# A hand-ordered mixer: weight halves ahead of state work on VectorE, SiLUs and a logarithm moved on ScalarE

## The chip, the core and the metric

One core of one Trainium2 chip. The metric is the device time of one execution in microseconds (us); less is better. Engines are named as in the profile: PE is TensorE's matmul side, PEld its weight loads, DVE is VectorE, ACT is ScalarE, POOL is GpSimd, SP is SyncE, which issues nearly all DMAs.

## What is computed

One decoder layer on 264 columns, 256 tokens of a prompt and 8 samples of one token each, with a model width of 2048: a half-step FFN, a mixer, another half-step FFN and a gated per-layer embedding, each with its norms. All of it is fp32. The change lies in the mixer:

```python
proj = u @ w_in                       # 2048 -> 81 column tiles of 128
glu_a, glu_b, z, xbc, dt_raw = split(proj)
v = glu_a * sigmoid(glu_b)            # conv group, 1024 channels
v = silu(layernorm(causal_dwconv(v, width 31)))
xbc = silu(causal_dwconv(xbc, width 4))
xs, B, C = split(xbc)                 # 8 groups, 6 heads each, state 128
dt = softplus(dt_raw + bias)
y, h_new = ssd(xs, dt, a, B, C, d_skip, h0)   # chunked scan, chunks of 128
y = rmsnorm(y * silu(z)) per group
mix = concat(v, y) @ w_out
```

For the 8 samples `ssd` is one step from a given state h0 (128 x 1024 fp32 for each third of a group): the output needs the product of the old state with C, summed over the state.

## The kernel before

**Matmuls and weights.** Activations lie with the channels on the partitions and the 264 columns along the free dimension. An fp32 product is made of three products in the rounded format fp32r: `mm3` (L449-454) issues high weight x high activation (L451), high weight x low activation (L452) and low weight x high activation (L453). Weights come in units of 8 tiles of 128x128, 512 KB: `Weights.load` (L303) issues one DMA on SP into `wraw` (L325), ScalarE copies it, rounding, into the high half `whi` (L328), and VectorE subtracts to get the low half `wlo` (L338). A column tile of the mixer takes two units, called n_0 and n_8, and 48 matmuls. `wraw`, `whi` and `wlo` have four buffers each, and loads are made two column tiles ahead. So a DMA into `wraw` waits for VectorE's low half of the unit two column tiles earlier, and a high copy waits until PE has done its last L452 of the unit two column tiles earlier. Accumulators are PSUM tiles `acc` (5 buffers); other PSUM tiles are `ps` (3 buffers).

**The mixer** (L805-1241) loops over `IN_ORDER` (L1153): dt first, then for each of the eight groups the tiles C, B, three x and three z, and, in between, pairs gb and ga of the conv group. Beside the weights' halves VectorE and ScalarE do:

- `do_conv` (L921-936): short conv of a B, C or x tile out of its accumulator; ScalarE takes the first tap, VectorE three more, ScalarE the SiLU (L936). It also collects the last columns in `xo`.
- `do_glu` (L952-972): the sigmoid as Exp, Ln, Exp on ScalarE (L957-959), a product on VectorE, and 30 long taps on VectorE (`y<-v,vec,y`, L418), four of them queued after each tile of the loop (L1238-1240).
- old-state work: `load_state` (L1037-1039) brings h0 through SP into one of two buffers; `state_times_c` (L1041-1047) multiplies it by C (`h<-h,cbc`, L415) and sums it (`ych<-h`, L1047). The next load into a buffer waits for that sum. `load_cbc` (L1033) brings C, spread over the partitions, into a single buffer.
- `load_sums` (L990-1008) brings the running sums of dt for a group into `ab` and `ea` through SP (L996); `decays` (L1012-1021) makes twelve Relus and three Exps of them on ScalarE; `decay_cb` (L1049) multiplies them on VectorE (`ab<-ab,rr`).
- `ssd` (L1060-1111): PE transposes x and B (L1070, L1071), VectorE scales them (`xdt`, `xde`), PE makes the chunk states (L1087) and the outputs (L1102). `ssd_samples` (L1114) does the samples.
- `gate_begin` (L1132): product with SiLU(z), three squares on ScalarE, two run additions on VectorE. `gate_end` (L1140-1147): PE sums over the partitions (L512), ScalarE takes the inverse root as Ln and Exp (`rsqrt`, L515-518), VectorE makes three outputs, and `split` (L456-465) makes of each a high half on ScalarE (L460) and a low half on VectorE (L461).
- the SiLU of a z tile (L1221) reads an accumulator and frees it. SiLU lies in another activation table than Ln and Exp; a change of table shows as ACT_TABLE_LOAD (L437).

**The order.** From the mixer's beginning on, each engine's order is written out by hand in `ISSUE` (L148-260): four lists, for PE, DVE, Activation and SP, of the engine's instructions by their place in the program. `issue_in_order` (L263-297) ties each instruction to the one before it in its list, without a semaphore. An engine works through its list in order, and an instruction that waits holds back all behind it.

## Time and profile before

| | us |
| --- | --- |
| time, median of 3 runs | 2380.87 |
| lowest and highest run | 2376.16, 2381.4 |
| the profiled execution | 2377.88 |
| its span | 2376.2 |
| PE busy in the span | 2355.9 |
| DVE busy | 1574.8 |
| ACT busy | 1187.7 |

The profile is one execution, and its times count from the start of the span; the mixer lies at about 822 to 1310 us. Rows of a timeline give the start, the duration of the group, engine and line, the operation with its tiles, how many follow one another, and in brackets the idle time before it and what ended it. A row of the waits names the engine and line that waited, the one that released it, the total, how often, and the longest. L-numbers are those of the kernel before.

### The profile page before, as it was taken

Reading aid. Unit: us, or ns where it says so; the run is one execution under the profiler, and the core shown is the slowest. Engines: PE = TensorE matmul, PEld = TensorE weight load, DVE = VectorE, ACT = ScalarE, POOL = GpSimd, SP = SyncE. Lnnn points to the kernel's source line nnn. Section 1 sums busy time; section 2 is a strip of 40 time slices with the busy share of each in tenths; the row PEclk is TensorE's granted clock in tenths of the full one; section 3 lists DMA queues with packets and bytes.
Section 4 is the critical chain, followed back from the end, with each engine's and each line's share of the span. In section 5 each row is a group of like instructions: output and inputs, shape, how many; then the busy total and the mean of one; then the engine's idle time right before and its main releaser. Section 6 shows DMA issues by size and latency. Waiting matters only on the chain.

```text
span 2376.2 us, 47323 instructions
## 1 busy us (share of the span) xinstructions
PE 2355.9 (99%) x19470; PEld 2335.6 (98%) x19470; DVE 1574.8 (66%) x2396; ACT 1187.7 (50%) x1791; POOL 184.7 (8%) x206
## 2 busy tenths in 40 slices
PE   9999999999999999999999999999999999999998
PEld 9999999999999999999999999999999999999998
DVE  6554455545556988989899965865545655565586
ACT  6444444433446576666565454644444443344465
POOL 1400000000006000000000011000000000000103
PEclk9999999999999999999999999999999999999999
DMA  7655555555555777666665556567766676676563
GB/s 261 218 185 181 185 183 182 184 183 184 184 171 184 232 240 227 211 226 208 226 215 188 185 170 230 186 239 244 237 202 228 232 245 212 214 237 207 180 207 126
DMA packets 163145, 489.34 MB, mean 206 GB/s; under 512 B 25280, under 2 KB 42736, under 8 KB 162928
## 3 DMA queue, kind: packets, MB, share of 16 engines
q1 hardware_dynamic: 160848, 485.27, 62.2%
q8 instruction: 152, 2.49, 0.4%
q10 hardware_dynamic: 2080, 1.04, 0.2%
q14 instruction: 65, 0.53, 0.1%
HBM read 465.65 MB, written 21.88 MB: 205 GB/s over the span
## 4 chain that ended last, share of the span: by engine, by line
PE 87%; DVE 7%; DMA 3%; ACT 2%; issue 1%; SPq 0%; ACTq 0%; DVEq 0%
PE acc L453 28%; PE acc L452 28%; PE acc L451 28%; DVE wlo L338 3%; DMA wraw<-in_w 2%; ACT whi L328 1%; DVE h L415 1%; PE ps L451 1%; PE ps L453 1%; PE ps L452 1%; DVE y L418 0%; DVE h L418 0%; PE ps L512 0%; PE ps L1102 0%; DMA ea<-d_cs 0%
## 5 line engine op out<-in xcount | busy, mean ns | idle before, releaser
L453 PE MATMUL acc<-act,wlo 128*128 128x264 f32 x6128 | 1733.5, 285 | 3.2 <-DVE wlo L338 3.2
L452 PE MATMUL acc<-act,whi 128*128 128x264 f32 x6128 | 1721.5, 282 | 1.8 <-DVE act L418 1.8
L451 PE MATMUL acc<-act,whi 128*128 128x264 f32 x6128 | 1704.4, 282 | 3.5 <-ACT whi L328 1.7
L338 DVE TENSOR_TENSOR wlo<-wraw,whi 128x1024 fp32r<-128x1024 f32 (+2 forms) x814 | 972.6, 1197 | 579.3 <-ACT whi L328 575.3
L328 ACT CAST whi<-wraw 128x1024 fp32r<-128x1024 f32 (+2 forms) x814 | 830.9, 1024 | 948.7 <-PE acc L452 662.4
L451 PEld LDWEIGHTS acc<-act,whi 128*128 128x128 f32 x6128 | 1147.1, 189 | 6.3 <-ACT whi L328 2.1
L453 PEld LDWEIGHTS acc<-act,wlo 128*128 128x128 f32 x6128 | 1145.6, 187 | 6.8 <-DVE wlo L338 4.8
L452 PEld LDWEIGHTS acc<-act,whi 128*128 128x128 f32 x6128 | 1147.1, 187 | 4.4 <-DVE act L418 2.2
L415 POOL TENSOR_TENSOR run<-run,tmp 128x264 f32<-128x264 f32 x77 | 72.9, 954 | 878.7 <-ACT tmp L442 878.3
L418 DVE SCALAR_TENSOR_TENSOR y<-v,vec,y 128x229 f32<-128x229 f32 (+21 forms) x240 | 106.9, 468 | 0.6
L418 DVE SCALAR_TENSOR_TENSOR s<-bb,xds,s 128x128 f32<-128x128 f32 x192 | 52.6, 346 | 69.7 <-POOL s L415 69.7
L415 POOL TENSOR_TENSOR s<-s,eap 128x1024 f32<-128x1024 f32 x24 | 46.4, 1935 | 630.6 <-DMA s<-in_hst 532.9
L415 DVE TENSOR_TENSOR tmp<-acc,rr 128x264 f32<-128x264 f32 x99 | 42.5, 430 | 48.9 <-PE acc L453 48.6
L460 ACT CAST act<-tmp 128x264 fp32r<-128x264 f32 x104 | 42.1, 410 | 63.0 <-DVE tmp L415 57.4
L415 DVE TENSOR_TENSOR tmp<-tmp,acc 128x264 f32<-128x264 f32 x84 | 35.9, 427 | 38.1 <-PE acc L453 37.9
L415 POOL TENSOR_TENSOR run<-run,y 128x264 f32<-128x264 f32 x7 | 8.4, 1207 | 582.9 <-ACT run L495 503.5
L415 DVE TENSOR_TENSOR y<-y,acc 128x264 f32<-128x264 f32 x80 | 34.0, 425 | 29.5 <-PE acc L453 29.5
L415 DVE TENSOR_TENSOR act<-tmp,act 128x264 fp32r<-128x264 f32 x122 | 52.9, 438 | 0.1
L453 PE MATMUL ps<-act,wlo 128*128 128x264 f32 x192 | 52.2, 284 | 0.0
L442 ACT ACTIVATE tmp<-tmp 128x264 f32<-128x264 f32 x112 | 46.9, 420 | 10.2 <-DVE tmp L415 9.9
L452 PE MATMUL ps<-act,whi 128*128 128x264 f32 x192 | 52.0, 282 | 0.0
L451 PE MATMUL ps<-act,whi 128*128 128x264 f32 x192 | 46.1, 282 | 0.0
(173 smaller groups left out, 1013.4 us busy)
## 6 DMA issues: line engine op xcount, KB each, us to landing
wraw<-in_w SPq DMA_DIRECT2D x755, 512.0 KB, 4.7
h<-in_hst SPq DMA_DIRECT2D x24, 512.0 KB, 8.1
s<-in_hst SPq DMA_DIRECT2D x24, 512.0 KB, 6.3
out_nss<-s SPq DMA_DIRECT2D x24, 512.0 KB, 2.6
wraw<-in_w SPq DMA_DIRECT2D x35, 256.0 KB, 3.8
wraw<-in_w SPq DMA_DIRECT2D x23, 384.0 KB, 7.3
ab<-d_cs SPq DMA_DIRECT2D x14, 384.0 KB, 5.5
cbc<-d_bc SPq DMA_DIRECT2D x8, 512.0 KB, 6.3
```

The source lines that it names most:

```text
L328: self.hi = nc.scalar.copy(hi, raw).ins
L338: nc.vector.tensor_tensor(out=lo, in0=raw, in1=hi.bitcast(F32), op=ALU.subtract)
L415: return (eng or nc.vector).tensor_tensor(out=out, in0=in0, in1=in1, op=op)
L418: return nc.vector.scalar_tensor_tensor(out=out, in0=in0, scalar=scalar, in1=in1, op0=op0, op1=op1)
L442: i = nc.scalar.activation(out=out, in_=in_, func=func, bias=bias, scale=scale)
L451: keep(nc.tensor.matmul(acc, hi, x[:, 0, :], start=first, stop=False))
L452: keep(nc.tensor.matmul(acc, hi, x[:, 1, :], start=False, stop=False))
L453: traced[0] = keep(nc.tensor.matmul(acc, lo, x[:, 0, :], start=False, stop=last)).ins
L460: nc.scalar.copy(t[:, 0, :], x)
```

## The change

Only two of the four lists in `ISSUE` change: DVE's (772 instructions) and Activation's (582). Each holds the same instructions as before in another order; PE's and SP's lists, buffers, tiles and arithmetic stay.

On DVE about seventy low weight halves move forward by 0.4 to 3.0 us of work, past products and sums of the old state, long taps and low halves of the gate's outputs. The sums and products that they pass come correspondingly later: for example sum 304 stands behind run addition 293 and low half 324 (173_8), where it stood ahead of 313, 316, 318 and 271; low half 440 (184_0) passes 381 and sum 417, but stays behind 379, the low half of the gate's first output; and the first `xde` of group 1 (141) passes 118, 120, 152 and 122.

On Activation two places change. In group 1 the first two z SiLUs (140, 143) go ahead of the table load 116 and of the copies and squares behind it, and the rsqrt (117, 118), table load 126 and third z SiLU (146) go ahead of the high copy of 161_8 (156). In group 4 the high halves of the gate's three outputs (299, 300, 301), which stood among the glu's Exp (308), the decays' Exps (318, 325, 326), table load 329 and high copies 340 and 341, go behind the high copy of 185_8 (347), and the SiLU 330 goes ahead of 341.

```diff
 "DVE":
-        57 76 60 81 83 74 77 80 59 61-62 89 82 90 84 91 94 85 78 111-112 63 113 116 64 131 92 95
-        86 79 132-133 136 114 154 93 65-66 96 67 87 134 137 115 155 99 98 173 88 135 68-69 156
-        159-160 174 107 100 164 70 157 175 108 101 158 176-177 109 102 110 103 127 104 138 161
-        128 178-179 105-106 180 129 181 184 162 188 130 182 189 163 150 183 123 125 117 119 121
-        166 165 151 139-140 124 126 190 193 118 120 152 122 141 202 191 153 203 192 171 204
...
+        57 76 60 77 80 59 61-62 81 83 89 74 90-91 94 78 111 82 112 84-85 63 113 116 64 131 92 79
+        132 95 86 133 136 114 154 93 65-67 134 115 155 96 87 99 98 173 137 135 68-69 156 159 174
+        88 160 107 100 164 70 157 175 108 101 158 176-177 109 102 110 103 127 104 138 161 178
+        128 179 105-106 180-181 184 188 129 162 182 189 130 163 150 183 123 125 117 119 121 166
+        165 151 139-140 124 126 190 193 141 202 118 120 191 203 152 122 192 204 153 171 142-143
...
-        245 256 300 250 342 246 257 301 251 311 264 252 265 253 266 292 267 312 303 317 323 270
-        304 313 316 318 271 293 314 324-325 328 349 329 272 294 315 350-351 354 326 355 330 273
...
+        300 250 342 246 301 251 311 257 264 252 265 253 266 292 267 312 303 317 323 313 316 293
+        314 324 270 304 325 328 349 318 294 315 350 271 329 272 351 354 326 355-356 330 273 352
...
-        376-377 402 404 395 400-401 396 399 410 397 378 380 382 411 416 398 412 415 379 388 403
-        405 381 417 413 440 383 441-442 445 431 389-390 414 450-451 443 391 456 430 444 392 457
...
+        376-377 396 399 410 400 397 378 380 382 411 401 416 398 412 415 379 388 403 405 413 440
+        381 441 417 442 445 431 389 414 450-451 383 390 443 456 391 430 444 392 457 418-419 393
...
-        435 482 493 458 474 483 485 459 494 499 486 460 495 498 500 475 461 505 496 476 464 506
...
+        426 448 427 471 449 428 472 479 452 432 524 453 433 480 454 434 481 484 435 482 493 455
+        474 483 494 458 485 459 499 495 498 475 505 486 460 496 476 506 500 507 510 497 531 461
...
 "Activation":
-        116 145 147 91-93 148-150 155-157 117-118 126 140 143 146 158 151 119-121 128 166 129
+        140 143 116 145 147 91-93 148-150 155 117-118 126 146 156-158 151 119-121 128 166 129
...
-        331 298 306 332-334 307 299 308 318 325 300 326 329 340 301 341-342 346 330 343 347 309
-        349 335 350 344 348 351-352 336-337 353-354 338 355-358 339 363 359 345 364-366 374-381
+        331 298 306 332-334 307-308 318 325-326 329 340 330 341-342 346 343 347 299-301 309 349
+        335 350 344 348 351-352 336-337 353-354 338 355-358 339 363 359 345 364-366 374-381
```

## The prediction, made before the changed kernel was run

> **What bounds the kernel now.** I read the page first, then the chain of waits of TensorE over the mixer, the only part whose orders change, then windows around each wait, then the instructions of VectorE, ScalarE and SP in those windows.

> ```profile
> PE 2355.9 (99%) x19470; PEld 2335.6 (98%) x19470; DVE 1574.8 (66%) x2396; ACT 1187.7 (50%) x1791; POOL 184.7 (8%) x206
> ```

> TensorE (PE) works 99% of a span of 2376.2 us, so no reordering on the other engines can win more than what TensorE now waits for. Which of it lies in the mixer, 822 to 1310 us, the waits say (engine, line, released by: us in total, times, longest):

> ```profile
> PE acc L453 <- DVE wlo L338: 2.5, 4, 0.9
> PE acc L451 <- ACT h L442: 1.6, 2, 1.3
> PE ps L1070 <- ACT tmp L442: 1.4, 1, 1.4
> PE ps L1070 <- ACT h L442: 1.3, 1, 1.3
> PE ps L512 <- DVE run L415: 0.4, 1, 0.4
> PE ps L1087 <- DVE xde L415: 0.4, 1, 0.4
> PE acc L451 <- ACT whi L328: 0.2, 1, 0.2
> ```

> They sum to 7.8 us, 0.33% of the time. That is the ceiling of any gain. Against it stands how full VectorE is where they lie (window, us, then busy us of PE, PEld, DVE, ACT, POOL, clock, DMA share, GB/s):

> ```profile
> 860.00:936.00 76.00, 72.52 (x589) 69.43 (x588) 74.31 (x130) 52.05 (x91) 0.00 (x0) 1.00 0.72 225
> ...
> 1003.00:1031.00 28.00, 27.28 (x226) 27.01 (x225) 28.00 (x49) 19.26 (x34) 0.00 (x0) 1.00 0.57 180
> ...
> 1063.00:1092.00 29.00, 26.99 (x224) 26.57 (x223) 28.41 (x47) 20.31 (x41) 0.00 (x0) 1.00 0.55 185
> ```

> VectorE is busy 74.31 of 76, 28.00 of 28 and 28.41 of 29 us. In these three stretches a microsecond that VectorE idles is a microsecond that everything behind it comes later, so a move is judged by one question: does the instruction that now comes first have its input?

> **The change, group by group.** Nothing is added or removed; each term is a wait that goes or a wait that comes. The sum is made on the profiled execution (2377.88 us), which is 3.0 below the median of the runs, 2380.87.

> *Group 1 (860 to 936).* Gain: the first two z SiLUs free their accumulators ahead of a table load, and the rsqrt stands ahead of a weight copy, so the waits of 1.4 (L1070) and 1.3 (L451) go, and the xde wait of 0.4 too. Loss: the low halves pushed forward stand ahead of the reduce that frees a state buffer.

> ```profile
> 887.46 1.21 DVE L1047 TENSOR_REDUCE ych<-h 128x8 f32<-128x1024 f32 x1
> ```
> ```profile
> 888.69 0.33 SPq L1039 DMA_DIRECT2D h<-in_hst  x1
> 890.62 0.97 SPq L996 DMA_DIRECT2D ab<-d_cs  x2
> ```
> ```profile
> 896.01 3.63 ACT L442 ACTIVATE ab<-ab,acs 128x128 f32<-128x128 f32 x12 [2.65 <-DMA ab<-d_cs]
> 899.54 1.04 ACT L328 CAST whi<-wraw 128x1024 fp32r<-128x1024 f32 x1
> ```
> ```profile
> 901.26 0.28 PE L451 MATMUL acc<-act,whi 128*128 128x264 f32 x1
> ```

> SP issues in order. The state load left at 888.69, right after the reduce ended at 888.67, and the ab loads behind it at 890.62. In the new order the work put ahead of the reduce, less that put behind, is 2.3 us. Low 132 (155_8) among it now also waits for weights that stand on SP behind another later state load, 1.4 us by my estimate (0 at least). The reduce ends near 892.5, the ab loads leave 2.3 later, since they had 1.6 us to spare behind the state load, and the twelve Relus, which already waited for them, start at 898.3. The copy behind them, high half 158_0, ends at 902.9 in place of 900.58. PE wants it at 901.26: +1.7, and VectorE, whose low 158_0 reads it, is 2.3 late. Then the moved high copy:

> ```profile
> 915.43 0.61 PE L512 MATMUL ps<-run,ones 128*128 128x264 f32 x2
> 915.87 0.61 PE L1054 MATMUL ps<-c,b 128*128 128x128 f32 x4
> ```
> ```profile
> 918.50 1.28 ACT L437 ACT_TABLE_LOAD   x1
> ```
> ```profile
> 918.36 1.22 DVE L338 TENSOR_TENSOR wlo<-wraw,whi 128x1024 fp32r<-128x1024 f32 x1
> ```

> The copy of 161_8 now stands behind the rsqrt, the table load and a SiLU. The rsqrt reads the sum of L512, which ends at 916.04 and so at 917.7 with PE 1.7 late; two steps of the rsqrt and a SiLU (some 0.4 each by my estimate, from the Relus' 12 in 3.63 and their longer tiles), 1.3 for the load and 1.04 for the copy give 921.3. Its low half starts there and not at 918.36: VectorE is now 2.9 late. The full stretch doesn't give it back before the second xde, whose work ahead is the same:

> ```profile
> 933.47 0.55 DVE L415 TENSOR_TENSOR xde<-xdt,dte 128x384 f32<-128x384 f32 x1
> ```
> ```profile
> 935.76 0.81 PE L1087 MATMUL ps<-xde,rr 128*128 128x384 f32 x2
> ```

> It ended at 934.02 and PE used it at 935.76, a slack of 1.74. With 2.9 it ends at 936.9, so **+1.2** at the end of the group, although the old waits are gone. Its bounds: with 0 in place of 1.4, the xde is only 1.5 late and the group gives 0.2 back; if nothing ahead is late, PE gains no more than the slack, −1.75; with another 0.5 of idle it is +1.75. I take +1.2.

> *Group 3 (1003 to 1031).* The low half 173_8 (VectorE 324) goes 3 us forward, past reduces, and would end the wait at 1010.94 (0.72 of the 2.5). But a run addition (293) stays ahead of it:

> ```profile
> 1008.05 0.72 ACT L442 ACTIVATE tmp<-h 128x264 f32<-128x264 f32 x2
> ```
> ```profile
> 1009.67 1.21 DVE L338 TENSOR_TENSOR wlo<-wraw,whi 128x1024 fp32r<-128x1024 f32 x1
> ```

> That addition reads the first of the two squares, done at about 1008.46. VectorE comes to it some 2.4 us earlier, once the reduces no longer stand before it, and idles. The low half ends near 1010.45 against 1010.88: 0.4 won of 0.7. The reduce that had let a state load go at 1007.07 (next fence) now comes behind it and one long tap: 0.4 and 1.2 more, so it ends at 1012.0. On it hangs the next state load, and on that, in SP's order, the weights:

> ```profile
> 1007.07 0.33 SPq L1039 DMA_DIRECT2D h<-in_hst  x1
> 1007.50 0.38 SPq L931 DMA_DIRECT2D out_xo<-xo  x1
> 1007.93 4.96 SPq L325 DMA_DIRECT2D wraw<-in_w  x3
> ```
> ```profile
> 1013.98 1.05 ACT L328 CAST whi<-wraw 128x1024 fp32r<-128x1024 f32 x1 [4.67 <-PE acc L453]
> ```
> ```profile
> 1017.62 0.28 PE L451 MATMUL acc<-act,whi 128*128 128x264 f32 x1
> ```

> Both move 4.9 us. The weights for 175_0 leave at 1012.9 instead of 1007.93. The copy began 6.05 after the issue, now at 1018.9, and ends at 1020.0 where PE wants it at 1017.62: **+2.4**. If they land in the median 4.7 us, it is +1.0; if the low half after it also queues behind a product that waits for the late state, +3.3.

> ```profile
> wraw<-in_w SPq DMA_DIRECT2D x755, 512.0 KB, 4.7
> ```

> [...]

> *Group 4 (1063 to 1092).* Gain: the SiLU that PE's transposes wait for (1.3) comes earlier, and low 184_0 (440) goes ahead of a reduce. But the three high copies of the gate (ScalarE 299 to 301, L460) now stand behind the high copy of 185_8 (347), and VectorE's subtraction (379) that reads the first of them still stands ahead of 440:

> ```profile
> 1078.39 0.28 PE L452 MATMUL acc<-act,whi 128*128 128x264 f32 x1
> ```
> ```profile
> 1076.17 0.42 DVE L415 TENSOR_TENSOR act<-tmp,act 128x264 fp32r<-128x264 f32 x1
> 1076.52 0.42 DVE L415 TENSOR_TENSOR v<-v,acc 128x264 f32<-128x264 f32 x1
> 1076.86 1.82 DVE L415 TENSOR_TENSOR ab<-ab,rr 128x768 f32<-128x768 f32 x2
> ```
> ```profile
> 1081.72 0.39 PE L453 MATMUL acc<-act,wlo 128*128 128x264 f32 x1 [0.74 <-DVE wlo L338]
> ```

> 347 writes the buffer that PE last reads at 1078.39, so it runs from about 1078.7 to 1079.7; the gate's copy (a quarter as wide: some 0.4 by estimate) ends at 1080.1. Only then do 379 (pitch 0.35), the v product (0.35), the two decay products (0.9 each), a conv tap (0.4) and low 440 (1.2) run: 1084.1. PE, which got it at 1081.72, gets it **2.4 later**, in one wait of 4 to 5 us from 1079.3 on. If 347 ran a microsecond earlier it would be +1.4; it can't run before its buffer is free, so this term has the firmest sign of the three. ScalarE and VectorE have nothing that could step in between, since each runs its list in order.

> *Group 5 (near 1127).* Low 191_0 goes 3 us forward past old-state work; the 0.9 wait goes, and the lows behind have over a microsecond of slack: **−0.9**.

> *All else* (group 2, 1130 on): the state loads that move have weights behind them with slack, or nothing that PE waits for; 0, within 0.5 either way. The 0.4 of L512 stays.

> Sum: +1.2 + 2.4 + 2.4 − 0.9 = **+5.1 us**, so 2383.0 for an execution like the profiled one and 2386.0 for the median. About 0.2% (4.8 us) is what a measurement here can tell from no change.

> **The rivals.** *The waits cancel.* The queued loads land in the median time (group 3 at +1.0), low 132 doesn't wait (group 1 at −0.2), group 4 at +1.4 to +2.4: with −0.9 the sum is +1.3 to +2.3, and 2382 to 2383. For it: both are estimates of how a queue catches up. Against it: DMA share in group 1 is already 0.72.

> *The lows do go first: faster.* If each moved low finds its input, the run addition of group 3 has its square in time and the gate's copy stands where 347 is already done, then the waits of groups 1, 3, 4 and 5 go without successors: 1.75 (the cap of the xde) + 0.7 + 1.3 + 0.7 + 0.9 = 5.4, so 2375.5. It decides at 1078: is there a high copy 347 before PE leaves that buffer? The rows say no, so this keeps a small chance.

> *The long wait costs more than itself.* TensorE's first matmuls, after it had stood still, went slowly:

> ```profile
> 1.56 4.29 PE L549 MATMUL ps<-ident,ones 128*128 128x128 f32 x24 [1.56 <-POOL ident masks.py:199]
> ```

> 24 took 4.29 us; at the pace of the four of L1054 (0.61, of which about 0.28, as in the rows of single matmuls above, is the last one's own length, so 0.11 apart) they would take 2.8. If the wait of 4 to 5 us in group 4 brings that on again, it adds about 1.5: 2387.5. Against it: after the waits of up to 1.4 us here the windows show a clock of 1.00; no row of the mixer shows a wait of 4.

> [...]

> **How the numbers follow.** My sum (+3 to +8): 0.51, of which 0.42 beyond 4.8. The cancelling: 0.28, of which 0.27 within 0.2%. The clean gain: 0.12, of which 0.10 beyond. The clock: 0.09, all slower. Slower 0.51, same 0.38, faster 0.11. The likeliest is 2386.0. The low end takes in the cancelling and most of the spread of three runs (2376.16 to 2381.4): 2377; the high end is every upper bound together (1.75 + 3.3 + 2.4 − 0.9 + 0.5 = 7.1) and the clock's 1.5, 2389.5, with half of that spread: 2392.

> **What would show it.** Right: a PE wait of 4 to 5 us on wlo L338 ending near 1084, with VectorE idle before a subtraction of L415 that ScalarE's L460 ends; the state load at about 1012 on SP and PE waiting on whi L328 near 1017; another such wait near 901; and no waits left at 918, 920, 1127. Wrong: group 4 without that idle, or weights for 175_0 leaving by 1009, or the twelve Relus still starting at 896.

## The result and the profile after

| us | before | changed |
| --- | --- | --- |
| median of 9 runs each | 2379.15 | 2386.59 |
| lowest to highest | 2374.8 to 2386.1 | 2384.35 to 2391.79 |
| span of the profiled execution | 2376.2 | 2384.0 |

The ratio is 1.0032, 95% interval 1.0018 to 1.0045: the changed kernel is 7.6 us slower (4.3 to 10.7).

What TensorE waited for in the mixer of the changed kernel (822 to 1320 us; line, released by: total, times, longest):

```profile
PE acc L453 <- DVE wlo L338: 3.7, 5, 2.7
PE acc L451 <- ACT whi L328: 3.4, 3, 2.0
PE ps L1087 <- DVE xde L415: 2.7, 2, 1.9
PE acc L451 <- DVE v L415: 1.8, 1, 1.8
PE ps L512 <- DVE run L415: 0.8, 1, 0.8
PE acc L451 <- ACT h L442: 0.6, 1, 0.6
```

13.0 us in place of 7.8. The old waits for `tmp` and `h` at the transposes (L1070) are gone. In their place stand high halves, the two xde's and a product `v`. Where they lie, from TensorE's timeline:

```profile
902.49 0.39 PE L451 MATMUL acc<-act,whi 128*128 128x264 f32 x1 [1.95 <-ACT whi L328]
```
```profile
931.99 0.88 PE L1087 MATMUL ps<-xde,rr 128*128 128x384 f32 x2 [1.86 <-DVE xde L415]
938.81 0.91 PE L1087 MATMUL ps<-xde,rr 128*128 128x384 f32 x2 [0.88 <-DVE xde L415]
```
```profile
1022.73 0.39 PE L451 MATMUL acc<-act,whi 128*128 128x264 f32 x1 [1.06 <-ACT whi L328]
```
```profile
1066.75 0.68 PE L512 MATMUL ps<-run,ones 128*128 128x264 f32 x2 [0.84 <-DVE run L415]
```
```profile
1087.62 0.36 PE L451 MATMUL acc<-act,whi 128*128 128x264 f32 x1 [1.76 <-DVE v L415]
1087.82 0.28 PE L452 MATMUL acc<-act,whi 128*128 128x264 f32 x1
1090.79 0.58 PE L453 MATMUL acc<-act,wlo 128*128 128x264 f32 x1 [2.69 <-DVE wlo L338]
```

And what the waits don't show: behind two of them TensorE ran at half its clock. The columns are the window, its length, busy TensorE, granted clock, DMA share and GB/s:

```profile
902.40:904.40 2.00, 1.91 (x11) 0.67 0.11 34
904.40:906.60 2.20, 2.20 (x12) 0.52 0.72 227
906.60:908.60 2.00, 2.00 (x18) 1.00 0.61 190
```
```profile
1090.00:1092.00 2.00, 1.21 (x5) 0.71 0.09 12
1092.00:1094.00 2.00, 2.00 (x11) 0.50 0.87 303
1094.00:1096.00 2.00, 2.00 (x18) 0.94 0.59 197
```

Matmuls start 0.22 us apart there instead of 0.12, for 3.3 us each time. "Busy" doesn't show it; the clock column does.

The best account sets the start of one matmul in one profile against its start in the other. The lead of before, by which the changed kernel starts the same matmul later, is 0.0 us at 860, 3.2 at 936, 3.3 at 1003, 5.5 at 1031, 6.6 at 1063, 10.6 at 1092, 9.5 at 1130, 8.9 at 1310 and 7.8 at the end. The last step back isn't the change's: between 1965 and 2190 that one execution of before lost 2.2 us, which no other execution here lost, not even another one of before (`before_again`).

### The profile page after: what moved, and what is told of

The parts are those of the page before. It is cut to its first block, busy times and chain, and to the rows that moved or that the text cites. A ratio compares the mean times of both kernels' runs of the same rounds, so it can differ in the third digit from the quotient of the medians.

```text
span 2384.0 us, 47322 instructions
## 1 busy us (share of the span) xinstructions
PE 2358.7 (99%) x19470; PEld 2337.3 (98%) x19470; DVE 1578.1 (66%) x2396; ACT 1188.7 (50%) x1791; POOL 184.7 (8%) x206
## 3 DMA queue, kind: packets, MB, share of 16 engines
q10 hardware_dynamic: 2080, 1.04, 0.1%
## 4 chain that ended last, share of the span: by engine, by line
PE 89%; DVE 5%; DMA 2%; ACT 1%; issue 1%; SPq 0%; POOL 0%; DVEq 0%; ACTq 0%; POOLq 0%
PE acc L451 29%; PE acc L452 28%; PE acc L453 28%; DVE wlo L338 2%; DMA wraw<-in_w 1%; ACT whi L328 1%; PE ps L451 1%; PE ps L452 1%; PE ps L453 1%; DVE h L415 1%; PE ps L512 0%; DVE h L418 0%; DVE y L418 0%; DMA s<-in_hst 0%; PE ps L1102 0%
## 5 line engine op out<-in xcount | busy, mean ns | idle before, releaser
L453 PE MATMUL acc<-act,wlo 128*128 128x264 f32 x6128 | 1734.1, 285 | 4.4 <-DVE wlo L338 4.4
L452 PE MATMUL acc<-act,whi 128*128 128x264 f32 x6128 | 1720.9, 282 | 1.8 <-DVE act L418 1.8
L451 PE MATMUL acc<-act,whi 128*128 128x264 f32 x6128 | 1705.9, 282 | 6.8 <-ACT whi L328 4.0
L338 DVE TENSOR_TENSOR wlo<-wraw,whi 128x1024 fp32r<-128x1024 f32 (+2 forms) x814 | 973.8, 1198 | 582.3 <-ACT whi L328 577.8
L328 ACT CAST whi<-wraw 128x1024 fp32r<-128x1024 f32 (+2 forms) x814 | 830.8, 1024 | 958.9 <-PE acc L452 685.6
L451 PEld LDWEIGHTS acc<-act,whi 128*128 128x128 f32 x6128 | 1148.8, 189 | 10.8 <-ACT whi L328 5.5
L453 PEld LDWEIGHTS acc<-act,wlo 128*128 128x128 f32 x6128 | 1146.3, 187 | 8.1 <-DVE wlo L338 6.2
L452 PEld LDWEIGHTS acc<-act,whi 128*128 128x128 f32 x6128 | 1148.2, 187 | 4.5 <-DVE act L418 2.2
L415 POOL TENSOR_TENSOR run<-run,tmp 128x264 f32<-128x264 f32 x77 | 72.9, 953 | 878.3 <-ACT tmp L442 877.8
L418 DVE SCALAR_TENSOR_TENSOR y<-v,vec,y 128x255 f32<-128x255 f32 (+28 forms) x240 | 107.8, 472 | 0.9
L415 POOL TENSOR_TENSOR s<-s,eap 128x1024 f32<-128x1024 f32 x24 | 47.2, 1967 | 629.4 <-DMA s<-in_hst 505.1
L415 DVE TENSOR_TENSOR tmp<-acc,rr 128x264 f32<-128x264 f32 x99 | 42.5, 430 | 50.1 <-PE acc L453 50.1
L460 ACT CAST act<-tmp 128x264 fp32r<-128x264 f32 x104 | 41.9, 410 | 54.6 <-DVE tmp L415 53.2
L415 DVE TENSOR_TENSOR tmp<-tmp,acc 128x264 f32<-128x264 f32 x84 | 35.9, 427 | 37.9 <-PE acc L453 37.9
L415 DVE TENSOR_TENSOR act<-tmp,act 128x264 fp32r<-128x264 f32 x122 | 53.0, 439 | 5.9 <-ACT act L460 5.8
L415 POOL TENSOR_TENSOR run<-run,y 128x264 f32<-128x264 f32 x7 | 7.1, 1020 | 593.2 <-ACT run L495 512.5
L415 DVE TENSOR_TENSOR y<-y,acc 128x264 f32<-128x264 f32 x80 | 33.9, 424 | 28.8 <-PE acc L453 28.8
L453 PE MATMUL ps<-act,wlo 128*128 128x264 f32 x192 | 52.2, 284 | 0.0
L452 PE MATMUL ps<-act,whi 128*128 128x264 f32 x192 | 52.0, 282 | 0.0
L442 ACT ACTIVATE tmp<-tmp 128x264 f32<-128x264 f32 x112 | 46.9, 420 | 8.6 <-DVE tmp L415 8.4
L451 PE MATMUL ps<-act,whi 128*128 128x264 f32 x192 | 46.1, 282 | 0.0
## 6 DMA issues: line engine op xcount, KB each, us to landing
wraw<-in_w SPq DMA_DIRECT2D x755, 512.0 KB, 4.6
h<-in_hst SPq DMA_DIRECT2D x24, 512.0 KB, 7.6
s<-in_hst SPq DMA_DIRECT2D x24, 512.0 KB, 7.1
out_nss<-s SPq DMA_DIRECT2D x24, 512.0 KB, 2.8
cbc<-d_bc SPq DMA_DIRECT2D x8, 512.0 KB, 6.6
```

Of the source, the lines that this page charges most:

```text
L328: self.hi = nc.scalar.copy(hi, raw).ins
L338: nc.vector.tensor_tensor(out=lo, in0=raw, in1=hi.bitcast(F32), op=ALU.subtract)
L415: return (eng or nc.vector).tensor_tensor(out=out, in0=in0, in1=in1, op=op)
L418: return nc.vector.scalar_tensor_tensor(out=out, in0=in0, scalar=scalar, in1=in1, op0=op0, op1=op1)
L442: i = nc.scalar.activation(out=out, in_=in_, func=func, bias=bias, scale=scale)
L451: keep(nc.tensor.matmul(acc, hi, x[:, 0, :], start=first, stop=False))
```

## The experiments

All of them change only the order lists, except where said. "Later" and "earlier" are starts of the same matmul against the profile of before.

**ScalarE's three copies back in place** (`copies_back`), all else as changed.

```diff
-        307-308 318 325-326 329 340 330 341-342 346 343 347 299-301
+        307 299 308 318 325 300 326 329 340 301 330 341-342 346 343 347
```

> The changed kernel with one part undone: ScalarE's 299, 300 and 301 (the high halves of the gate's outputs) stand again among the Exps, ahead of high copy 347; everything else as changed. Theory A (waits at three places, and two spells at half the TensorE clock behind long waits): the 5.8 us idle of VectorE before 379 and the PE waits of 1.8 and 2.7 us near 1088 go, and so does the half clock behind them (1.5 us). From group 4's start to its end the kernel was 4.0 us later than before the change; now it should be 1.4 to 2 us earlier there, so about 5 us faster than the changed kernel and 2 to 3 us slower than before. Rival B (the loss is VectorE's late sums in groups 1 and 3 alone, and what is lost in group 4 is their late state loads arriving): group 4 keeps most of its waits, and the kernel stays 6 us or more slower than before.

Measured: ratio to before 1.0006 (0.9996 to 1.0016), so 1.4 us slower than before and 6 faster than the changed kernel. Group 4 (1063 to 1092) is 2.5 us shorter than before, with no PE wait in it. VectorE's rows of 379, the subtraction that reads the first of those copies, in the changed kernel and here:

```profile
1086.70 0.43 DVE L415 TENSOR_TENSOR act<-tmp,act 128x264 fp32r<-128x264 f32 x1 [5.79 <-ACT act L460]
```
```profile
1080.18 0.43 DVE L415 TENSOR_TENSOR act<-tmp,act 128x264 fp32r<-128x264 f32 x1
```

The idle of 5.79 us is made by the place of those three copies. The low halves moved ahead in group 4 are a gain once it is gone. Rival B falls: group 4 kept none of its waits. Groups 1 to 3 keep theirs: at 1031 this execution is 5.4 us behind before, with a wait of 2.72 for a high half at 1021 and half clock behind it (the granted clock of its whole span is 0.998).

**Those three copies alone, on the kernel before** (`copies_late_alone`).

```diff
-        307 299 308 318 325 300 326 329 340 301 341-342 346 330 343 347
+        307-308 318 325-326 329 340-342 346 330 343 347 299-301
```

> The kernel before with one move alone: ScalarE's 299, 300 and 301 behind high copy 347. Theory A: VectorE idles 3.5 to 5 us before 379 until ScalarE's copy, low 440 (which here also stands behind 381 and sum 417) ends 4 us later, PE waits 4 us or more in one piece near 1080 and then runs at half clock for 3.3 us: +5 to +6.5 us in all, two thirds of it wait. Rival E (the half clock comes from load or temperature, not from the wait): +4 us, with the clock at 1.00 behind the wait.

Measured: 1.0024 (1.0013 to 1.0036), +5.7 us. Group 4 alone makes 6.0 us: PE waits 1.67 for `v` and 4.22 for the low half, so the wait came in two pieces and not in one. The clock behind it:

```profile
1083.80:1088.40 4.60, 0.38 (x3) 0.74 0.05 7
1088.40:1090.40 2.00, 2.00 (x9) 0.50 0.48 150
1090.40:1092.80 2.40, 2.40 (x13) 0.50 0.80 280
1092.80:1095.00 2.20, 2.20 (x20) 0.99 0.71 203
```

Rival E falls: the half clock sets in during the wait and ends 4.5 us after it. In this execution it also followed before's own waits near 920 (2.02 and 1.28); the granted clock of its whole span is 0.998.

**ScalarE's list alone** (`act_alone`): VectorE's list of before.

```diff
-    "DVE": the changed list
+    "DVE": the list before
```

> ScalarE's list as changed, VectorE's as before. Theory A: group 1 gains (both PE waits near 918 go, but the second xde, whose low halves wait for the late copy of 161_8, caps it: between -1.7 and 0), group 3 is as before, group 4 loses more than in the changed kernel, since low 440 stands behind 381 and the sum 417 too: a PE wait of 5 to 7 us there with 1.5 us of half clock behind it, +5 to +6. In all +3.5 to +6 us. Rival B (VectorE's sums make the loss, ScalarE's moves gain): faster than before by 1 to 3 us.

Measured: 1.0019 (1.0008 to 1.003), +4.5 us. Group 1 gains 0.1, group 4 loses 5.4 with waits of 1.76 and 4.16 and a spell of half clock (matmuls 0.22 us apart from 1084.60 to 1087.24). Rival B falls here too.

**VectorE's list alone** (`dve_alone`): ScalarE's list of before.

```diff
-    "Activation": the changed list
+    "Activation": the list before
```

> VectorE's list as changed, ScalarE's as before. Theory A: the ab loads leave late and PE waits about 2 us for high half 158_0 near 901, with or without half a clock behind it (1.7); the state load of group 3 leaves near 1012 to 1016 instead of 1007 (+2); group 4 gains 0.5 to 1.5 and group 5 about 1.0, 1174 another 0.6. In all +1 to +4 us. Rival C (VectorE's low halves ahead are a gain everywhere, the loss is ScalarE's alone): faster than before by 1.5 us or more.

Measured: 1.0010 (1.0000 to 1.0019), +2.4 us. Against before, groups 1 and 3 lose 5.1 and 2.5 us, group 4 wins 2.5 and the rest of the mixer 1.7. Rival C falls: a low half ahead isn't a gain everywhere. In group 1, PE's old wait for the rsqrt even grew, that for the SiLU stayed, and half clock from 921.7 to 928.5 followed, but none behind the first of these three waits:

```profile
902.98 0.39 PE L451 MATMUL acc<-act,whi 128*128 128x264 f32 x1 [2.24 <-ACT whi L328]
```
```profile
920.50 0.55 PE L1070 MATMUL ps<-ident,h 128*128 128x128 f32 x3 [1.95 <-ACT tmp L442]
922.65 0.59 PE L451 MATMUL acc<-act,whi 128*128 128x264 f32 x1 [1.28 <-ACT h L442]
```

**VectorE's order of groups 1 and 3 as before, all else as changed** (`groups13_back`).

```diff
-        314 324 270 304 325 328 349 318 294 315 350 271 329 272 351 354 326 355-356 330 273 352
+        304 313 316 318 271 293 314 324-325 328 349 329 272 294 315 350-351 354 326 355 330 273
...
```

> The changed kernel with VectorE's order of groups 1 and 3 as before (sums ahead of the low halves again); group 2, groups 4 on and ScalarE's list as changed. Theory A: the wait near 902 goes with its half clock, as do the late loads near 1016; group 1 ends 0 to 1.5 us earlier than before instead of 3.1 later, group 3 adds nothing; group 4 still loses about 4 with its half clock, groups 5 on win 1.6. In all 1 to 3 us slower than before and 5 us faster than the changed kernel. Rival G (late sums cost nothing, the whole loss is in group 4): no more than 1.5 us faster than the changed kernel.

Measured: 1.0015 (1.0005 to 1.0025), +3.6 us and so 4 faster than the changed kernel. The wait near 902 is gone and group 3 adds nothing. Rival G falls by the profile: at 1031 this execution is 1.5 us behind before, where the changed one was 5.5. By the times alone it is less sure, since the two intervals overlap. But group 1 itself ends 1.7 us later than before, where I expected it 0 to 1.5 earlier, by a PE wait of 2.9 for the xde and half clock behind it (the granted clock of its whole span is 0.998); so the whole is 3.6 and not 1 to 3 slower than before.

**Group 1's ScalarE moves alone, on the kernel before** (`silus_alone`).

```diff
-        116 145 147 91-93 148-150 155-157 117-118 126 140 143 146 158
+        140 143 116 145 147 91-93 148-150 155 117-118 126 146 156-158
```

> The kernel before with group 1's ScalarE moves alone (two z SiLUs early, the copy of 161_8 behind the rsqrt, the table load and the third z SiLU). Theory A: PE's waits of 1.4 and 1.3 near 918 to 920 go, but low 161_8 waits for its copy and the second xde ends 1 to 1.5 us later, so PE waits there: 0 to 1.5 us faster. Rival F (the moved SiLUs give their whole 2.7): 2.5 us faster or more.

Measured: 1.0000 (0.9991 to 1.0010). One wait has taken the place of two:

```profile
930.97 0.88 PE L1087 MATMUL ps<-xde,rr 128*128 128x384 f32 x2 [2.89 <-DVE xde L415]
```

Rival F falls. The 2.7 us at the transposes and the SiLU are bought with 2.9 at the xde, with half clock behind it in this execution (matmuls 0.22 us apart from 931.98 on).

**Only the moves that nothing later pays for** (`kept_gains`).

```diff
 DVE, on the list before up to 368, then the changed list
-        118 120 152 122 141 202 191 153 203 192 171 204 142
+        141 202 118 120 191 203 152 142 122 192 204 153 171
-        81 83 74 77 80 59 61-62
+        77 80 59 61-62 81 83 74
-        379 388 403 405 413 440
+        379 388 403 440 405 413
 Activation, on the list before
-        116 145 147 91-93 148-150 155-157 117-118 126 140 143 146
+        140 143 116 145 147 91-93 148-150 155 117-118 156-157 126 146
-        340 301 341-342 346 330 343 347
+        340 330 301 341-342 346 343 347
```

> Only the moves that no later instruction pays for. ScalarE: the two z SiLUs ahead of the table load and the rsqrt ahead of the copy of 161_8, but that copy ahead of the third z SiLU's table load; SiLU 330 ahead of 301 and 341; 299 to 301 otherwise in place. VectorE: before's order up to group 4, but the xde's ahead of products, long taps and low halves of the gate; in group 4 low 440 right behind the first decay product; from group 4 on the changed order. Theory A: PE's waits of 0.4 (870), 1.4 and 1.3 (918, 920), 1.3 (1080), most of 0.7 (1082), 0.9 (1128) and 0.4 (1175) go with nothing in their place: 5 to 6.5 us faster than before, with a granted clock of 1.000. Rival D (each wait that goes comes back somewhere later, since VectorE is full): within 2 us of before.

Measured: 0.9978 (0.9968 to 0.9988), 5.2 us faster than before, with the clock at 1.000. But not by the sum I had made. PE is 2.0 us ahead at the end of group 1, and 1.5 behind at 1031: groups 2 and 3 take 3.3 back. So rival D is right for these groups. It wins 2.5 in group 4 and 1.7 behind it, and it has no half clock, which the kernel before has in some executions (below). All in all this profile is 2.7 us ahead of before's at the mixer's end, half of the 5.2. The other half goes with the clock: where the granted clock of the whole span reads 1.000, nine executions of this kernel average 2373.2 and seven of before 2375.8, 2.6 us apart. That half clock alone makes up the rest is argued.

**Four places for the small rows** (`kept_rows4` on `kept_gains`, `before_rows4` on the kernel before). What held group 3 in `kept_gains`: ScalarE's copy of the transposed C (L1028) waits until the 4 KB DMA that reads the buffer's last content is done, with high copies queued behind it. The first line is of before, the second of `kept_gains`:

```profile
ACT rows L1028 <- DMA d_bc<-rows: 12.6, 4, 3.6
```
```profile
ACT rows L1028 <- DMA d_bc<-rows: 14.6, 5, 4.8
```

The edit lets four copies lie in four ranges of partitions of one tile:

```diff
-        rows = mp.tile([P, P], F32, tag="rows", bufs=1, name=nm("rows"))
-        nc.scalar.copy(rows[:NS], pr[:NS])
+        at = 32 * ((2 * g + i) % 4)
+        nc.scalar.copy(rows4[at : at + NS], pr[:NS])
```

> The list of moves that were kept (kept_gains), and besides the rows of C and B for the samples, which one buffer held, in four different rows of partitions, so that ScalarE's copy (L1028) doesn't wait until the 4 KB DMA of the copy before it is done. Theory A (in kept_gains the 2.1 us won in group 1 were given back in groups 2 and 3, because ScalarE stood 4.8 us in that copy at 993 to 998 with two high copies behind it): the wait of that copy goes, PE's wait of 1.3 for whi at 1008 goes, and the kernel is 1 to 2 us faster than kept_gains, 6 to 8 us faster than before. Rival D (PE, once early, meets the weights' DMA anyway): no more than 0.5 us faster than kept_gains, with the PE waits for whi in the same place, released by wraw.

Measured: 0.9976 (0.9966 to 0.9987), median 2372.3, lowest to highest 2371.02 to 2373.61. That wait is gone, and PE's wait for whi at 1008 with it; PE is 1.6 us ahead of before at 1031 where `kept_gains` was 1.5 behind. Of the 3.0 us that it was ahead at 936, groups 2 and 3 still take 1.4 back, so a part of rival D stays. What is left of PE's waits in the mixer:

```profile
PE acc L453 <- DVE wlo L338: 1.4, 3, 0.6
PE ps L512 <- DVE run L415: 0.9, 1, 0.9
PE acc L451 <- ACT h L442: 0.6, 1, 0.6
PE ps L1089 <- DVE xde L415: 0.5, 1, 0.5
```

3.4 us in place of 7.8 (L1089 is L1087 moved by two lines). The mechanism of theory A is shown by the waits. Its size isn't: I had expected 1 to 2 us over `kept_gains`, and in time the two can't be told apart (0.5 us between the medians, with different runs of before beside them).

> The kernel before with the same four places for the rows and nothing else. Theory A: ScalarE's wait of 3 to 3.6 us in that copy goes, but PE isn't waiting for it there: within 1 us of before. If the rows' DMA alone bound groups 2 to 4, it would be 2 us faster or more.

Measured: 0.9992 (0.9983 to 1.0001), a gain of 1.9 us at best guess and not clear of none. ScalarE's wait is gone, PE's waits are not (8.4 us in the mixer). Nothing in its profile shows a gain. Whether it is within 1 us of before or 2 us faster stays open.

**The two kernels once more under the profiler** (`after_again`, `before_again`), without a change.

> The changed kernel, once more under the profiler. Theory A: PE's waits near 902, 932, 1023 and 1088 to 1091 come back within 0.3 us of their lengths, since the order makes them. Whether half clock follows a wait of about 2 us differs between executions if it hangs on where the wait falls in a fixed span of time; behind the 1.8 and 2.7 us near 1088 it follows again. If it follows the same waits as before in all places, it is a matter of length alone.

Measured: 2388.44 us. The waits come back at the same places, two of them longer by more than I allowed for: 2.40 at 905 (it was 1.95) and 2.03 at 1024 (1.06). Half clock followed in group 4 again (0.50 from 1093.1 to 1095.4). It followed the wait at 1024, too, and did not follow the one at 905, though that was longer this time. The granted clock right behind 905, then behind 1024:

```profile
905.40:907.40 2.00, 2.00 (x17) 1.00 0.09 26
```
```profile
1024.40:1027.20 2.80, 2.80 (x14) 0.50 0.58 196
```

> The kernel before, once more under the profiler. PE's waits of 1.3 to 1.4 near 918, 920 and 1080 come back. Theory A: the two near 918 and 920, 2.7 us together, may be followed by half clock in this execution though they weren't in the other, and the 2.1 us that the other execution lost between 1965 and 2190, as no other kernel here did, aren't lost again.

Measured: 2377.39 us. The waits of 1.31 and 1.28 at 917 and 920, which no half clock had followed in the profile shown ahead of the prediction, were followed by one now, and so was a pair of under 1 us each near 1080 and 1082:

```profile
920.00:923.00 3.00, 3.00 (x16) 0.50 0.73 191
```
```profile
1083.60:1086.80 3.20, 3.20 (x16) 0.50 0.84 287
```

And the 2.2 us between 1965 and 2190 weren't lost again.

## Why the prediction was right, and where its sum was off

| place | forecast | measured, us |
| --- | --- | --- |
| group 1 | +1.2 | +3.2: 1.5 of waits, 1.7 of half clock |
| groups 2 and 3 | +2.4 | +2.4 |
| 1031 to 1063 | 0 | +1.1 |
| group 4 | +2.4 | +4.0: 2.5 of waits, 1.5 of half clock |
| group 5 | −0.9 | −1.2 |
| 1130 to 1310 | 0 | −0.6 |
| the rest | 0 | −1.1: −2.2 by that execution of before, and +1.1 mostly at the out projection, where the kernels here lie 0 to 2.3 later |
| sum | +5.1 | +7.8; by the medians' ratio 7.6 |

The forecast time, 2386.0, came so near the measured 2386.59 partly by luck: it stood on a median of three runs of before, 1.7 us above that of the nine, and its sum was 2.5 us short.

*Group 1.* The chain came as written, its steps within 1.3 us. In the changed profile, SP's rows and ScalarE's:

```profile
891.52 0.33 SPq L1039 DMA_DIRECT2D h<-in_hst  x1
891.94 0.97 SPq L996 DMA_DIRECT2D ab<-d_cs  x2
```
```profile
897.15 1.87 ACT L442 ACTIVATE ab<-ab,acs 128x128 f32<-128x128 f32 x6 [4.67 <-DMA ab<-d_cs]
899.64 1.86 ACT L442 ACTIVATE ab<-ab,acs 128x128 f32<-128x128 f32 x6 [0.62 <-DMA ab<-d_cs]
901.41 1.03 ACT L328 CAST whi<-wraw 128x1024 fp32r<-128x1024 f32 x1
```

The state load left at 891.5 (forecast 892.5), the ab loads right behind it, and the copy of 158_0 ended at 902.44 (902.9). PE's waits near 918 went. VectorE idled 2.65 before low 161_8, which stood for the "2.9 late", and both xde's became PE's waits. I had put the cap at the second xde; the first took most of it.

*Group 3.* The state load left at 1015.86 and the weights at 1016.72. Taken back by the 3.8 us that PE was late there, that is 1012.0 and 1012.9, as written:

```profile
1015.86 0.33 SPq L1039 DMA_DIRECT2D h<-in_hst  x1
1016.28 0.38 SPq L931 DMA_DIRECT2D out_xo<-xo  x1
1016.72 9.08 SPq L325 DMA_DIRECT2D wraw<-in_w  x6
```

The run addition kept low 173_8 waiting (1.55 us before it, for the square). The weights were copied 4.9 us after their issue and not 6.05, so that wait is 1.06 and not 2.4. Smaller ones (0.36 for whi at 1010.80, 0.20 and 0.18 for low halves at 1014 and 1017) made up for it: the sum of group 3 was right partly by luck.

*Group 4.* Shown by itself in two experiments. The wait was forecast as one of 4 to 5 us and came as 1.76 and 2.69, the first for the `v` product (388), which frees an accumulator and stands behind 379 too. I had listed that product in the queue and not looked at who waits for it. The end came where it was forecast: taken back by the 6.6 us that PE was late there, VectorE's idle ends at 1080.1 (forecast 1080.1) and PE goes on at 1084.2 (forecast 1084.1).

*1031 to 1063*, a step that I had put at 0: PE waits for run additions (L512), which stand behind a low half that waits 3.59 us for ScalarE. ScalarE stood 5.16 us in the copy of the rows, with SP's loads later than before. That the rows' DMA holds that copy is shown by `kept_rows4`; that it makes this wait here is argued.

*The clock* is the step that failed. I gave half clock a chance of 0.09, behind one wait of 4 to 5 us, for 1.5 us. It cost that much there (1.5), and 1.7 more behind the wait of 1.95 near 902, which I had forecast as 1.7 with no half clock behind it. With both (3.2) the forecast sum would have been 8.3 against 8.9 at the mixer's end. The reason that I gave against it, no drop behind waits of 1.4 us in one profile, was worth little: another execution of the same kernel drops behind them. What tells the cases of these traces apart isn't the length alone but how much of a wait falls into one stretch of 3.41 us (TensorE was busy for 1.46 us of the stretch ahead of the spell at 903.09, and for 1.82 of the one near 932 that no spell followed); the last section works this out.

## What to carry to other kernels

Ahead of moving an instruction forward on an engine that is full, look at what it reads: if its input isn't there, the whole queue waits with it (here 5.79 us on VectorE, behind one subtraction), and what it passes (a sum that frees a buffer, a copy that another engine reads) comes late. That isn't always paid for: in `kept_gains` low half 440 of group 4 still passes the sum 417, and PE has no wait there between 1013 and 1310, so what counts is whether what was passed had time to spare. Follow such a delay through SP, where one late state load held the weights behind it (1015.86 and 1016.72 in the changed profile, 1007.07 and 1007.93 before). And count PE's waits twice: by their length, and by what the clock may take behind them (1.7 and 1.5 us here). The kernel with the shortest waits here was steadier as well (2371.0 to 2373.6 for the best one, 2373.8 to 2381.1 for the kernel before beside it).

## What the runs showed of the hardware

```profile
899.68:903.09 3.41, 1.46 (x13) 1.00 0.79 300
903.09:906.50 3.41, 3.41 (x18) 0.50 0.46 143
930.39:933.81 3.42, 1.82 (x12) 1.00 0.02 5
```

And in `after_again`, where the wait of 2.40 is cut in two by the grid and that of 2.03 isn't:

```profile
901.05:904.46 3.41, 1.90 (x16) 1.00 0.98 379
904.46:907.87 3.41, 2.52 (x21) 1.00 0.30 79
1020.51:1023.93 3.42, 1.42 (x12) 1.00 0.97 352
1023.93:1027.34 3.41, 3.38 (x15) 0.50 0.67 226
```

Behind every one of the 15 stretches at full clock with up to 1.56 us busy, half clock began. With 1.61 to 1.82 it did in two of six, and above that in none. In these traces the border lies near half a stretch: one wait of 1.95 us (near 902 in the changed profile) was enough and one of 2.89 (928.5 in `act_alone`) went free; the pairs of 4.4 us or more in sum were followed by it all five times. A spell of 3.41 us with matmuls 0.22 us apart instead of 0.12 costs by these numbers an estimated 1.5 us.

A 4 KB store kept its buffer for 4.7 to 7.0 us in `kept_gains`, by the copies that waited for it: the longest was issued at 990.8, and the next copy into the buffer started at 997.8. Whether the weights' loads beside it make it so long was not tested.
